# A state-space layer on one Trainium2 core: chunk kernels built inside the input-product loop, TensorE in a fixed order up to the gated unit, outputs by quarters, last blocks singly

## The chip, the cores and the metric

The kernel runs on one core of one Trainium2 chip, in one launch. The metric is the device time of one execution in microseconds. Five engines run their own instruction streams in order and wait for one another through semaphores: TensorE (PE: matrix products and transposes into PSUM), VectorE (DVE), ScalarE (ACT), GpSimd (POOL) and SyncE (SP, which here only issues DMAs). The DMAs of SP's queue bring the weights from HBM into SBUF.

## The reference

Two model blocks follow each other on 256 tokens of width 1024 in float32. The first has a state-space layer with its feed-forward part, then an attention layer with another. The second (a time-mixing layer, a differential attention, attention to a memory) is not touched. What the change touches is the first layer of the first block:

```python
shift1, scale1, gate1, shift2, scale2, gate2 = jnp.split(c_act @ ada_w[l] + ada_b[l], 6, axis=-1)
h = modulate(rms_norm(x, norm1_g[l]), shift1, scale1)
# s5_mixer, 64 groups of 16 channels, each with a 64-wide complex diagonal state
#   s_t = A s_(t-1) + B u_t ;  y_t = Re(C s_t) + d_skip * u_t
y = (y + d_skip.astype(f32) * h.astype(f32)).astype(h.dtype)
g = jax.nn.gelu(y)
mix = g * jax.nn.sigmoid(g @ w_glu + b_glu)
x = x + gate1[:, None, :] * mix
h = modulate(rms_norm(x, norm2_g[l]), shift2, scale2)
x = x + gate2[:, None, :] * swiglu(h, ffn_w_gate[l], ffn_w_up[l], ffn_w_down[l])
```

`c` is one vector, so `c_act @ ada_w` is a product of a vector with a 1024 x 6144 matrix (24 MB): it costs loading, hardly any arithmetic.

## The kernel before, in words

The state-space layer (`s5`) works on chunks of eight tokens. Its steps, in the order of the code:

1. *Input products.* For eight group sets `e`, DVE and POOL multiply the input matrix with powers of A (tile `P`, DVE's stream of 128x512 products), PE transposes the eight blocks of `P` (into `Bm`) and multiplies them with the output matrix `cbd`, which gives the response of a chunk to itself, `KTr`, a part of tile `x`.
2. *Inputs.* `xs` (tokens) are multiplied by a modulation that comes from the first 2048 columns of `ada_w` (tiles `in_adaH`), transposed into `U`, and turned into each chunk's contribution to the state: `into` (products `Bm`·`U`, copy `Gs`) and `turnG` (transposes, copies into `GT`).
3. *Scan.* DVE adds up the states over the 32 chunks: `St[:, 1::8] <- GT[:, 0::8]` first, then a recurrence of 45 instructions.
4. *Chunk kernels.* For four pairs `i`: two transposes of `KTr` by matrix product, to which a product with a 16x128 matrix adds `d_skip`; a copy; a split into two float32r parts `kparts` (ACT casts, POOL subtracts); 14 products with a shift matrix; ACT copies into `Kmat`.
5. *Outputs.* 64 products `Kmat`·`U` and 256 products `CE`·`St` add up in four PSUM banks `psY`; a copy to `ys`; transposes; gelu (`gT`) and its two parts `gh`, `gl`.
6. *Gated unit.* `proj` multiplies `w_glu` (four tiles of 1 MB, each cut into parts `whi`, `wlo`) with `gh`, `gl`: three products for each of 8 x 8 blocks, 192 in all. `evac` applies sigmoid, gate and residual, and the sums of squares for the next norm follow.

**The weight queue.** All big weights come as 128x2048 tiles `raw` (1 MB) through SP's queue, in program order, into a ring of three buffers. `deepen(3)` adds three more buffers, `rawq`, after the pool `old` has been closed; they lie in its memory, which holds `GT`, `xs`, `P`, `s5bc` and the scan's temporaries `w`. So the first DMA into `rawq` must wait for the scan's last instruction, and SP, which is in order, holds all later tiles behind it.

**The filler.** The vector-matrix products are cut into steps; `self.pump()` issues the next one: four products `ps_gv <- raw, crep` on one tile. The list is: `in_adaH` (8 tiles), two sets of `in_ada` (8 tiles each), `in_kvada` (on DVE and POOL: `acc <- raw, cs`, 8 tiles, under `issue_after(self.after)`), `in_ada1`.

**Order.** Tile's scheduler orders each engine's instructions by a cost model. Inside `tc.manual_schedule(engines={PE})` PE keeps the order of the code; before the change this reaches from the loop of step 1 to the last `turnG`. The scheduler chooses all the rest, among it where steps 4 to 6 stand.

The later parts that the change touches: `normed` and `ffn` (the feed-forward part, whose `self.after` holds back the DVE products of `in_kvada`), and `down`, its last projection (22 x 8 blocks, also by `proj`).

Of the kernel before, what the change touches and what calls it, by code (L numbers as in the profile page):

```python
# [9 lines left out]
F32 = mybir.dt.float32  # L10
# [125 lines left out]
def pack(inp):  # L136
# [40 lines left out]
    d = i["s5_d"][0].reshape(4, 2, 8, 16).transpose(2, 0, 1, 3).reshape(64, 16)  # L177
    dm = np.zeros((16, 64, 16), np.float32)
    dm[np.arange(16), :, np.arange(16)] = d.T
    a["s5d"] = dm.reshape(16, 1024)  # L180
# [108 lines left out]
class K:  # L289
# [135 lines left out]
    def proj(self, get, n0, kb, obs, xh, xl, evac, every=0):  # L425

        n = n0
        for o in range(0, len(obs), 2):
            ps = self.ps()
            pair = obs[o:o + 2]  # L430
            for e, ob in enumerate(pair):
# [202 lines left out]
    def s5(self):  # L634
# [3 lines left out]
        with ExitStack() as ctx:  # L638
# [17 lines left out]
            dd = x0[0:16, 4:8]  # L656
            G.dma_start(out=dd.rearrange("p a t -> p (a t)"), in_=a["s5d"])

            dm = dd.rearrange("p a (g e) -> p (a g) e", e=16)
# [152 lines left out]
            for h in range(2):  # L812
# [4 lines left out]
                for j4 in range(2):  # L817
# [5 lines left out]
                    (S_.copy if j4 else V.tensor_copy)(out=o, in_=pt)  # L823

# [24 lines left out]
            self.pipe(4, [into, turnG])  # L849
            order.close()  # L850
# [3 lines left out]
            scp = self.ps()  # L854
# [4 lines left out]
            V.tensor_copy(out=St[:, 1::8], in_=GT[:, 0::8])  # L859
# [26 lines left out]
            shift = sm.tile([128, 256], F32R, tag="junk", name="shift")  # L886
            S_.copy(out=shift[:, :240], in_=c["shift"])

            with ExitStack():
                for i in range(4):  # L890
                    pt = self.ps("aux")
                    for j in range(2):
                        self.mm(pt[:, 128 * j:128 * j + 128], KTr[:, 2 * i + j, :], self.ident, True, False)
                        self.mm(pt[:, 128 * j:128 * j + 128], self.ident[0:16, :],
                                dm[:, 16 * i + 8 * j:16 * i + 8 * j + 8].rearrange("p g e -> p (g e)"), False, True)
                    k7 = KM[i][:, 7].rearrange("p j n -> p (j n)")
                    S_.copy(out=k7, in_=pt[:, :256])
                    self.pump()
                    kp = sm.tile([128, 2, 256], F32R, tag="pm", name="kparts", bufs=2)
                    self.split(kp[:, 0], kp[:, 1], k7, G)  # L900
                    for t2 in (5, 3, 1, 0):
                        if t2 == 1 or t2 == 3 and i < 2:
                            self.pump()
                        pt = self.ps("aux")
                        ts_ = [0] if t2 == 0 else [t2, t2 + 1]
                        for e, tt_ in enumerate(ts_):
                            k = 7 - tt_
                            for p in range(2):
                                self.mm(pt[:, 256 * e:256 * e + 256], shift[:, 112 - 16 * k:240 - 16 * k], kp[:, p], p == 0, p == 1)
# [1312 lines left out]
```

## Time and profile before

| | |
|---|---|
| runs (us) | 1085.94, 1090.19, 1091.70; median 1090.19 |
| profiled execution (us) | 1090.09, its span 1088.3 |
| mean granted TensorE clock | 0.981 of full |
| busy share of the span | PE 91%, DVE 75%, ACT 54%, POOL 25% |
| the state-space stage, start to first product of the gated unit | 0 to 113.1 us |
| gated unit's products | 113.1 to 137.5 us |
| feed-forward part begins on PE | 144.8 us |

The page has the busy time of the engines, the span in forty slices, the DMA queues, the chain of work that ended last and the costliest groups of instructions. A timeline row has start, duration, engine and line, what is written from what, and the idle time in front with its releaser. PE's rows include idle gaps of its pipeline only where a bracket says so. The time of the execution outside the span is 1090.09 - 1088.3 = 1.8 us.

### The profile page before, as it was taken

Reading aid. Unit: us, or ns where it says so; the run is one execution under the profiler, and the core shown is the slowest. Engines: PE = TensorE matmul, PEld = TensorE weight load, DVE = VectorE, ACT = ScalarE, POOL = GpSimd, SP = SyncE. Lnnn points to the kernel's source line nnn. Section 1 sums busy time; section 2 is a strip of 40 time slices with the busy share of each in tenths; the row PEclk is TensorE's granted clock in tenths of the full one; section 3 lists DMA queues with packets and bytes.
Section 4 is the critical chain, followed back from the end, with each engine's and each line's share of the span. In section 5 each row is a group of like instructions: output and inputs, shape, how many; then the busy total and the mean of one; then the engine's idle time right before and its main releaser. Section 6 shows DMA issues by size and latency. Waiting matters only on the chain.

```text
span 1088.3 us, 21333 instructions
## 1 busy us (share of the span) xinstructions
PE 989.6 (91%) x8162; PEld 883.6 (81%) x8162; DVE 818.4 (75%) x1762; ACT 585.3 (54%) x1299; POOL 268.9 (25%) x302
## 2 busy tenths in 40 slices
PE   3889979989999888989999999988897989899996
PEld 1346869989999866878999999988787886699984
DVE  8856689889996887779665554689687835686995
ACT  6334655555544767656555544665444344474663
POOL 7960100020011550100000011453214232243331
PEclk9999989999999988999999999999999999899999
DMA  7985648887885251256655553332211233174421
GB/s 277 374 318 229 260 154 346 329 321 298 307 340 221 101 186 43 78 194 245 226 188 195 194 178 135 126 126 83 83 41 45 98 117 107 54 260 162 149 79 39
DMA packets 29414, 198.78 MB, mean 183 GB/s; under 512 B 3744, under 2 KB 3872, under 8 KB 6528
## 3 DMA queue, kind: packets, MB, share of 16 engines
q1 hardware_dynamic: 27936, 191.73, 47.6%
q10 hardware_dynamic: 720, 3.15, 0.8%
q0 software_dynamic: 656, 2.53, 0.7%
q8 instruction: 64, 1.05, 0.4%
q14 instruction: 38, 0.31, 0.1%
HBM read 195.31 MB, written 2.10 MB: 181 GB/s over the span
## 4 chain that ended last, share of the span: by engine, by line
PE 66%; DVE 16%; POOL 7%; issue 4%; ACT 3%; DMA 2%; SPq 0%; POOLq 0%; DVEq 0%; ACTq 0%
PE ps_mm L327 50%; PE ps_aux L327 6%; POOL CE L306 3%; DVE wlo L306 3%; PE ps_sv L327 3%; PE ps_st L327 2%; PE ps_aux L330 2%; PE ps_el L327 2%; POOL cem L306 2%; DMA raw<-in_ada 1%; DVE acc L323 1%; ACT whi L376 1%; DVE A L306 1%; DMA raw<-in_kvada 1%; POOL sq L306 1%
## 5 line engine op out<-in xcount | busy, mean ns | idle before, releaser
L376 ACT CAST whi<-raw 128x512 fp32r<-128x512 f32 (+2 forms) x488 | 296.4, 613 | 272.2 <-PE ps_mm L327 230.7
L306 DVE TENSOR_TENSOR wlo<-raw,whi 128x512 fp32r<-128x512 f32 (+2 forms) x412 | 289.8, 716 | 127.4 <-ACT whi L376 123.7
L327 PE MATMUL ps_mm<-hh,whi 128*128 128x256 f32 x1064 | 306.7, 289 | 3.4 <-ACT hh L298 2.3
L327 PE MATMUL ps_mm<-hh,wlo 128*128 128x256 f32 x1064 | 299.6, 284 | 3.5 <-DVE wlo L306 3.5
L327 PE MATMUL ps_mm<-hl,whi 128*128 128x256 f32 x1064 | 300.0, 283 | 0.7 <-DVE hl L323 0.3
L327 PEld LDWEIGHTS ps_mm<-hh,whi 128*128 128x128 f32 x1064 | 201.9, 190 | 7.8 <-ACT hh L298 2.9
L327 PEld LDWEIGHTS ps_mm<-hh,wlo 128*128 128x128 f32 x1064 | 200.4, 189 | 7.6 <-DVE wlo L306 5.8
L327 PEld LDWEIGHTS ps_mm<-hl,whi 128*128 128x128 f32 x1064 | 201.6, 190 | 2.2 <-DVE hl L323 1.4
L306 POOL TENSOR_TENSOR wlo<-raw,whi 128x512 fp32r<-128x512 f32 (+2 forms) x76 | 101.4, 1335 | 250.8 <-ACT whi L376 220.7
L306 POOL TENSOR_TENSOR sq<-sq 128x256 f32<-128x256 f32 x20 | 22.1, 1103 | 396.4 <-ACT sq L298 246.1
L327 PE MATMUL ps_mm<-ah,wlo 128*128 128x256 f32 x352 | 99.0, 282 | 0.0
L327 PE MATMUL ps_mm<-ah,whi 128*128 128x256 f32 x352 | 99.0, 281 | 0.0
L327 PE MATMUL ps_mm<-al,whi 128*128 128x256 f32 x352 | 98.8, 281 | 0.0
L323 DVE SCALAR_TENSOR_TENSOR acc<-raw,cs,acc 128x512 f32<-128x512 f32 x112 | 79.8, 756 | 2.1 <-DMA raw<-in_kvada 1.2
L327 PEld LDWEIGHTS ps_mm<-ah,wlo 128*128 128x128 f32 x352 | 66.3, 189 | 2.5 <-issue 1.7
L327 PEld LDWEIGHTS ps_mm<-ah,whi 128*128 128x128 f32 x352 | 67.3, 191 | 0.1
L327 PEld LDWEIGHTS ps_mm<-al,whi 128*128 128x128 f32 x352 | 66.4, 189 | 0.0
L327 PE MATMUL ps_gv<-raw,crep 128*32 128x512 f32 x192 | 28.8, 677 | 22.5 <-DVE ps_mm L306 14.4
L327 PEld LDWEIGHTS ps_gv<-raw,crep 128*32 128x32 f32 x192 | 4.8, 115 | 28.3 <-DVE ps_mm L306 14.4
L327 PE MATMUL ps_mm<-whi,ch 128*128 128x512 f32 x48 | 20.0, 448 | 1.2 <-ACT ch L422 1.2
L306 POOL TENSOR_TENSOR CE<-CE,cem 128x512 f32<-128x512 f32 x16 | 20.3, 1294 | 0.0
L327 PE MATMUL ps_mm<-oh,whi 128*128 128x256 f32 x64 | 20.1, 314 | 0.0
(554 smaller groups left out, 2063.4 us busy)
## 6 DMA issues: line engine op xcount, KB each, us to landing
raw<-in_gu SPq DMA_DIRECT2D x44, 1024.0 KB, 5.9
raw<-in_ada SPq DMA_DIRECT2D x32, 1024.0 KB, 7.1
raw<-in_dn SPq DMA_DIRECT2D x22, 1024.0 KB, 5.0
raw<-in_win SPq DMA_DIRECT2D x15, 1024.0 KB, 4.8
raw<-in_adaH SPq DMA_DIRECT2D x8, 1024.0 KB, 7.7
raw<-in_kvada SPq DMA_DIRECT2D x8, 1024.0 KB, 6.0
raw<-in_ada1h SPq DMA_DIRECT2D x8, 1024.0 KB, 6.4
raw<-in_wout SPq DMA_DIRECT2D x8, 1024.0 KB, 4.9
```

The costliest lines, as they stand in the source:

```text
L306: return (eng or self.nc.vector).tensor_tensor(out=out, in0=a, in1=b, op=op)
L323: return self.nc.vector.scalar_tensor_tensor(out=out, in0=a, scalar=s, in1=b, op0=op0, op1=op1, **kw)
L327: return self.nc.tensor.matmul(out, l, r, start=start, stop=stop, **kw)
L330: return self.nc.tensor.transpose(out, in_, self.ident)
L376: i = self.nc.scalar.copy(out=hi[:, :width], in_=raw[:, o:o + width])
```

## The change

- **Chunk kernels** (`kernels(i)`) are made inside the loop over `e` and, for the last pair, between the transposes of `xs`. The split is ACT's cast and a DVE subtraction straight from PSUM (POOL before). `d_skip` is added while `KTr` is made, by one more product per `e`, from a 128x128 matrix.
- **PE's fixed order** reaches up to the second half of gelu. Pumps: one per `e`, one between the halves of `xs`, one after each step of `into`/`turnG`, and **eight between the products `Kmat`·`U`**, which stand after `deepen(3)`.
- **Scan**: the copy into `St` goes to ACT, the gelu table is loaded ahead of it (`self.table`), the small PSUM tile has another tag.
- **Outputs by quarters**: `outputs(0..2)`, `gelu(0)`, `outputs(3)`, `gelu(1)`.
- **proj**: with `coming`, the first pair of blocks is done `k` by `k`, its 16 weight blocks taken first; with `single` the last block gets its own PSUM tile, and the block before it is evacuated alone. The gated unit has both, `down` has `single`.
- **`self.after`** is the last `lo` of the norm (`self.lowed`), not the last `nrm`.

```diff
-    def proj(self, get, n0, kb, obs, xh, xl, evac, every=0):
+    def proj(self, get, n0, kb, obs, xh, xl, evac, every=0, coming=False, single=False):
...
+            if coming and not o:
+                w = [get(n + i) for i in range(2 * kb)]
+                n += 2 * kb
+                for k in range(kb):
+                    for e in range(2):
+                        self.mm3(ps[:, e * T:(e + 1) * T], *w[kb * e + k], xh(k), xl(k), k + e == 0, k + e == kb)
+            for e, ob in enumerate(pair if o or not coming else ()):
+                if e and single and o + 2 >= len(obs):
+                    evac(pair[0], ps[:, 0:T])
+                    ps, pair = self.ps(), pair[1:]
+                    e = 0
...
+            def kernels(i):
+                pt = self.ps("aux")
+                for j in range(2):
+                    self.T(pt[:, 128 * j:128 * j + 128], KTr[:, 2 * i + j, :])
+                kp = sm.tile([128, 2, 256], F32R, tag="pm", name="kparts", bufs=2)
+                S_.copy(out=kp[:, 0], in_=pt[:, :256])
+                self.sub(kp[:, 1], pt[:, :256], kp[:, 0].bitcast(F32))
+                S_.copy(out=KM[i][:, 7].rearrange("p j n -> p (j n)"), in_=pt[:, :256])
+                yield
+                for t2 in (5, 3, 1, 0):
...
+                            self.mm(pt[:, 256 * e:256 * e + 256], shift[:, 112 - 16 * k:240 - 16 * k], kp[:, p], p == 0, p == 1)
...
+                yield
...
-                        self.mm(o, cbd[:, r, 4 * e + q].rearrange("p b e -> p (b e)"), pv(r, q), r == 0, r == 1, (0, 32 * q))
+                        self.mm(o, cbd[:, r, 4 * e + q].rearrange("p b e -> p (b e)"), pv(r, q), r == 0, False, (0, 32 * q))
+                self.mm(psK[:, 0:16], self.ident, dd[:, e], False, True)
                 S_.copy(out=KTr[:, e], in_=psK[:, :128])
-                self.pump(2 if e % 3 == 1 else 1)
+                if e % 2:
+                    kern = kernels(e // 2)
+                elif kern:
+                    next(kern)
+                self.pump()
+                if e % 2:
+                    next(kern)
...
+                if not h:
+                    next(kern)
+                    self.pump()
...
-            self.pipe(4, [into, turnG])
-            order.close()
+            for _ in self.steps(4, [into, turnG]):
+                self.pump()
+            self.table(AF.Gelu_apprx_tanh)
...
-            scp = self.ps()
+            scp = self.ps("aux")
...
-            V.tensor_copy(out=St[:, 1::8], in_=GT[:, 0::8])
+            S_.copy(out=St[:, 1::8], in_=GT[:, 0::8])
...
             first.close()
...
+                    if jp % 2:
+                        self.pump()
...
+            for i in range(3):
+                outputs(i)
+            gelu(0)
+            outputs(3)
+            gelu(1)
+            order.close()
...
-            self.proj(self.stream(a["wglu"]), 0, 8, list(range(8)), lambda k: gh[:, k], lambda k: gl[:, k], evac, 24)
+            self.proj(glu, 0, 8, list(range(8)), lambda k: gh[:, k], lambda k: gl[:, k], evac, 24, True, True)
...
-                self.stt(lo[:, k], t, s, hi[:, k].bitcast(F32), ALU.add, ALU.subtract)
+                self.lowed = self.stt(lo[:, k], t, s, hi[:, k].bitcast(F32), ALU.add, ALU.subtract)
...
-            self.after = self.scaled
+            self.after = self.lowed
```

The block of chunk kernels that stood behind the scan (step 4) is removed, with its pumps; `deepen(3)` stands between `first.close()` and the products `Kmat`·`U`, as before.

First, PE at the end of step 2 and in step 5. Before the change, behind the last `turnG` (`Gs` is its source):

```order
L330 MATMUL ps_aux<-c_cst_75,Gs 128x128 x4
L327 MATMUL ps_aux<-c_cst_75,x 128x128
L327 MATMUL ps_aux<-x,c_cst_75 128x128
L327 MATMUL ps_aux<-c_cst_75,x 128x128
L327 MATMUL ps_aux<-x,c_cst_75 128x128
L327 MATMUL ps_gv<-raw,crep 32x512 x4
L327 MATMUL ps_aux<-kparts,shift 128x256 x14
L327 MATMUL ps_gv<-raw,crep 32x512 x4
```

And now, from the last of the products `Kmat`·`U` (the first of eight such rows has `Kmat_242`) to the first `CE`·`St`:

```order
L327 MATMUL ps_mm<-Kmat_242,U 32x128 x8
L327 MATMUL ps_gv<-raw,crep 32x512 x4
L327 MATMUL ps_mm<-Kmat_243,U 32x128 x8
L327 MATMUL ps_gv<-raw,crep 32x512 x4
L327 MATMUL ps_mm<-Kmat_244,U 32x128 x8
L327 MATMUL ps_gv<-raw,crep 32x512 x4
L327 MATMUL ps_mm<-Kmat_245,U 32x128 x8
L327 MATMUL ps_gv<-raw,crep 32x512 x4
L327 MATMUL ps_mm<-CE_659,St 32x128 x2
```

These are the last four of eight pumps; all eight stand ahead of the first product `CE`·`St`. Before the change no pump stands between the last `Kmat`·`U` and the first `CE`·`St`.

Second, SP's queue around the transfer of the residual input `x` (brackets: semaphores waited for; `DVE_49` is the scan's last instruction in the row that also names `Pool_49`). Before:

```order
L925 DMA x<-in_xT 128x2048 [waits DMASW2_49,PE_49,Activation_49]
L357 DMA raw<-in_wglu 128x2048 [waits DVE_49,Activation_49,Pool_49]
L357 DMA raw<-in_wglu 128x2048
L357 DMA raw<-in_ada 128x2048 [waits DMAHW0_49]
L357 DMA raw<-in_wglu 128x2048 [waits DMAHW1_49]
L357 DMA raw<-in_ada 128x2048 [waits DMAHW2_49]
```

Now:

```order
L357 DMA raw<-in_ada 128x2048 [waits DVE_49,Activation_49,Pool_49]
L357 DMA raw<-in_ada 128x2048 x2
L357 DMA raw<-in_ada 128x2048 [waits DMAHW2_49,PE_49]
L357 DMA raw<-in_ada 128x2048 [waits DMAHW3_49,DMAHW1_49,PE_49]
L357 DMA raw<-in_ada 128x2048 [waits DMAHW4_49,PE_49]
L357 DMA raw<-in_ada 128x2048 [waits DMAHW5_49,PE_49]
L357 DMA raw<-in_ada 128x2048 [waits DMAHW6_49,PE_49]
L357 DMA raw<-in_wglu 128x2048 [waits DMAHW7_49,PE_49]
L357 DMA raw<-in_wglu 128x2048 [waits DMAHW0_49,PE_49]
L357 DMA raw<-in_ada 128x2048 [waits DMAHW1_49,PE_49]
L357 DMA raw<-in_wglu 128x2048 [waits DMAHW2_49,PE_49]
```

The row that follows is a tile of `in_kvada`. Before, 14 of the 16 tiles of `in_ada` were issued ahead of the wait for the scan; now 7 are, and 9 behind it.

Third, DVE in the loop of step 1, from the last products `P` of the seventh `e` to the modulation. Before:

```order
L306 TENSOR_TENSOR P<-P,ps_mm 128x512 x2
L306 TENSOR_TENSOR ps_mm<-ps_mm,s5bc 128x512
L306 TENSOR_TENSOR P<-ps_mm,s5bc 128x512
L306 TENSOR_TENSOR ps_mm<-ps_mm,s5bc 128x512
L306 TENSOR_TENSOR P<-P,ps_mm 128x512 x2
L323 SCALAR_TENSOR_TENSOR ps_mm<-ps_mm,modH 128x256
L306 TENSOR_TENSOR xs<-xs,ps_mm 128x1024 x4
```

Now:

```order
L306 TENSOR_TENSOR P<-P,ps_mm 128x512 x2
L306 TENSOR_TENSOR kparts<-ps_aux,kparts 128x256 x2
L306 TENSOR_TENSOR ps_mm<-ps_mm,s5bc 128x512
L306 TENSOR_TENSOR P<-ps_mm,s5bc 128x512
L306 TENSOR_TENSOR ps_mm<-ps_mm,s5bc 128x512
L306 TENSOR_TENSOR P<-P,ps_mm 128x512 x2
L323 SCALAR_TENSOR_TENSOR ps_mm<-ps_mm,modH 128x256
L306 TENSOR_TENSOR xs<-xs,ps_mm 128x1024 x3
L306 TENSOR_TENSOR kparts<-ps_aux,kparts 128x256
```

The subtractions of the second and third pair stand together, ahead of the last `e`'s products; the third pair's source on PE stands behind 14 shift products of the second pair and two pumps.

## Rows read from the trace of the kernel before

**Rows 1.** Windows: busy us of the engines (instructions), PE clock, DMA share, GB/s.
```profile
24.00:48.00 24.00, 21.61 (x242) 10.71 (x234) 23.93 (x38) 11.66 (x29) 23.53 (x34) 1.00 0.89 331
97.00:102.00 5.00, 5.00 (x192) 5.00 (x188) 0.69 (x1) 2.29 (x4) 0.00 (x0) 1.00 1.01 424
102.00:107.00 5.00, 3.67 (x80) 2.77 (x73) 2.78 (x5) 1.94 (x3) 0.00 (x0) 1.00 1.00 418
107.00:112.00 5.00, 2.58 (x20) 1.04 (x16) 2.39 (x7) 4.92 (x13) 0.00 (x0) 0.90 1.01 416
113.10:137.50 24.40, 24.40 (x203) 24.37 (x200) 15.04 (x26) 13.51 (x27) 4.42 (x5) 0.97 0.60 235
150.00:160.00 10.00, 8.22 (x65) 7.61 (x65) 10.00 (x19) 6.07 (x10) 0.00 (x0) 1.00 0.55 193
```

**Rows 2.** DVE's timeline, end of step 1 to the scan.
```profile
39.87 1.27 DVE L306 TENSOR_TENSOR P<-P,ps_mm 128x512 f32<-128x512 f32 x2
...
42.86 1.27 DVE L306 TENSOR_TENSOR P<-P,ps_mm 128x512 f32<-128x512 f32 x2
44.05 0.42 DVE L323 SCALAR_TENSOR_TENSOR ps_mm<-ps_mm,modH 128x256 f32<-128x256 f32 x1
44.51 4.86 DVE L306 TENSOR_TENSOR xs<-xs,ps_mm 128x1024 f32<-128x1024 f32 x4
...
68.19 4.39 DVE L859 COPY St<-GT 128x256 f32<-128x256 f32 x1 [1.93 <-ACT GT L846]
72.61 0.43 DVE L306 TENSOR_TENSOR ps_mm<-St,ps_mm 128x256 f32<-128x256 f32 x1
...
78.97 0.18 DVE L306 TENSOR_TENSOR mods<-ps_aux,c_cols 128x16 f32<-128x16 f32 x1 [0.87 <-PE ps_aux L628]
...
93.68 1.27 DVE L306 TENSOR_TENSOR St<-St,w 128x448 f32<-128x448 f32 x2
```

**Rows 3.** PE's timeline, steps 1, 2 and 4 (an x8 of `ps_gv` is one pump).
```profile
42.14 0.66 PE L327 MATMUL ps_aux<-P,cbd 128*32 128x128 f32 x16
42.67 1.07 PE L327 MATMUL ps_gv<-raw,crep 128*32 128x512 f32 x8
43.67 1.09 PE L330 MATMUL ps_aux<-c_cst,P 128*128 128x128 f32 x8
...
55.24 1.28 PE L327 MATMUL ps_aux<-Bm,U 128*32 128x128 f32 x32
...
62.84 1.06 PE L327 MATMUL ps_gv<-raw,crep 128*32 128x512 f32 x8 [1.05 <-DMA raw<-in_ada]
...
80.30 2.17 PE L327 MATMUL ps_aux<-kparts,shift 128*128 128x256 f32 x14
```

**Rows 4.** ACT's timeline: last GT copy, a small copy and cast, first weight part, table.
```profile
67.12 1.03 ACT L846 COPY GT<-ps_aux 128x256 f32<-128x256 f32 x2 [1.52 <-PE ps_aux L330]
68.59 0.37 ACT L897 COPY Kmat<-ps_aux 128x256 f32<-128x256 f32 x1 [0.43 <-PE ps_aux L327]
69.00 0.40 ACT L422 CAST kparts<-Kmat 128x256 fp32r<-128x256 f32 x1
...
99.89 1.69 ACT L376 CAST whi<-raw 128x512 fp32r<-128x512 f32 x3 [0.71 <-DMA raw<-in_wglu]
...
106.26 1.28 ACT L298 ACT_TABLE_LOAD   x1
107.56 1.09 ACT L298 ACTIVATE gT<-ps_aux 128x512 f32<-128x512 f32 x2
```

**Rows 5.** SP's timeline, the tiles behind the scan.
```profile
95.03 1.23 SPq L357 DMA_DIRECT2D raw<-in_wglu  x2
```

**Rows 6.** PE's timeline, steps 5 and 6.
```profile
96.48 6.66 PE L327 MATMUL ps_mm<-CE,St 64*32 64x128 f32 x229
...
107.54 1.33 PE L330 MATMUL ps_aux<-c_cst,ys 128*128 128x128 f32 x8
111.27 1.93 PE L327 MATMUL ps_gv<-raw,crep 128*32 128x512 f32 x8 [2.40 <-DMA raw<-in_ada]
113.13 0.58 PE L327 MATMUL ps_mm<-gh,whi 128*128 128x256 f32 x1
```

**Rows 7.** Chain that ended last, steps 3 to 6 and behind (start, us, what).
```profile
70.46 1.28 POOL CE L306
...
97.33 13.89 DMA raw<-in_ada
...
137.46 0.85 ACT sg L298 x2
138.31 0.02 issue
138.33 0.43 DVE sg L306
138.76 0.58 DVE x L323
...
150.07 1.35 DVE acc L319 x4
151.42 0.23 issue
151.65 0.69 DVE wlo L306
```

More of the change, by code (lines that the diff above doesn't have):

```diff
@@ L175, in pack @@
     a["s5bc"] = np.concatenate([lay3(i["s5_b_re"][0]), lay3(i["s5_b_im"][0]), lay3(cc[0]), lay3(cc[1])], 1)
[L177 to L180, printed above, removed]
+    d = i["s5_d"][0].reshape(4, 2, 8, 16).transpose(0, 1, 3, 2)
+    dm = np.zeros((4, 2, 16, 8, 16), np.float32)
+    dm[:, :, np.arange(16), :, np.arange(16)] = d.transpose(2, 0, 1, 3)
+    a["s5d"] = dm.reshape(128, 128)
     a["wglu"] = _blocks(i["s5_w_glu"][0])
@@ L655, in s5 @@
             x0 = self.xp.tile([128, 8, T], F32, name="x")
-            dd = x0[0:16, 4:8]
-            G.dma_start(out=dd.rearrange("p a t -> p (a t)"), in_=a["s5d"])
-            dm = dd.rearrange("p a (g e) -> p (a g) e", e=16)
+            G.dma_start(out=x0[:, 4, 0:128], in_=a["s5d"])
+            dd = x0[:, 4, 0:128].rearrange("p (g e) -> p g e", g=8)
             box = []
@@ L766, in s5 @@
             KTr = x0[:, 0:4].rearrange("p a (b n) -> p (a b) n", b=2)
+            shift = sm.tile([128, 256], F32R, tag="junk", name="shift")
+            S_.copy(out=shift[:, :240], in_=c["shift"])
+            def kernels(i):
[8 more added lines that the diff above has]
+                for t2 in (5, 3, 1, 0):
+                    pt = self.ps("aux")
+                    ts_ = [0] if t2 == 0 else [t2, t2 + 1]
+                    for e, tt_ in enumerate(ts_):
+                        k = 7 - tt_
+                        for p in range(2):
+                            self.mm(pt[:, 256 * e:256 * e + 256], shift[:, 112 - 16 * k:240 - 16 * k], kp[:, p], p == 0, p == 1)
+                    S_.copy(out=KM[i][:, t2:t2 + len(ts_)].rearrange("p t j n -> p (t j n)"), in_=pt[:, :256 * len(ts_)])
+                yield
             order = ctx.enter_context(ExitStack())
@@ L885, in s5 @@
                 self.add(o, o, w1[:, 1])
[L886 to L909, printed above, removed]
-                        S_.copy(out=KM[i][:, t2:t2 + len(ts_)].rearrange("p t j n -> p (t j n)"), in_=pt[:, :256 * len(ts_)])
             first.close()
@@ L924, in s5, with outputs @@
                                     KM[jp // 2][:, :, jp % 2, 32 * q + 16 * b:32 * q + 16 * b + 16], jp % 4 == 0, False, (0, r))
+                    if jp % 2:
+                        self.pump()
             nc.sync.dma_start(out=x0, in_=a["xT"].rearrange("p (k t) -> p k t", k=8))
-            for q2 in range(2):
-                for jp in range(8):
-                    y = psY[2 * q2 + jp // 4]
+            ys = B8("U", [128, 2, 8, 8, 16], "ys")
+            gT = B8("C", [128, 8, 8, 32], "gT", 4)
+            gh = B8("C", [128, 8, T], "gh", 4, F32R)
+            gl = B8("C", [128, 8, T], "gl", 4, F32R)
+            self.wparts, self.npart = [((_W(big, 4), "A"), (_W(big, 4), "CE"))], 0
+            glu = self.stream(a["wglu"])
+            def outputs(i):
+                y = psY[i]
+                for jp in range(4 * (i % 2), 4 * (i % 2) + 4):
                     for qo in range(2):
-                        g = 4 * jp + 2 * q2 + qo
+                        g = 4 * jp + 2 * (i // 2) + qo
                         for ri in range(2):
@@ L936, in s5, with gelu @@
                                         False, jp % 4 == 3 and ri == 1, (64 * b, r))
-            ys = B8("U", [128, 2, 8, 8, 16], "ys")
-            for i, y in enumerate(psY):
                 o = ys[:, i // 2, :, 4 * (i % 2):4 * (i % 2) + 4].rearrange("p t j e -> p j t e")
                 (V.tensor_copy if i % 2 else S_.copy)(out=o, in_=y.rearrange("p (j t e) -> p j t e", j=4, t=8))
-            gT = B8("C", [128, 8, 8, 32], "gT", 4)
-            gh = B8("C", [128, 8, T], "gh", 4, F32R)
-            gl = B8("C", [128, 8, T], "gl", 4, F32R)
-            self.wparts, self.npart = [((_W(big, 4), "A"), (_W(big, 4), "CE"))], 0
-            for q2 in range(2):
+            def gelu(q2):
                 for t4 in range(2):
@@ L1112, in down @@
             def down():
-                self.proj(self.stream(self.a[f"dn{l}"]), 0, 22, list(range(8)), lambda k: ah[:, k], lambda k: al[:, k], evac, 12)
+                self.proj(self.stream(self.a[f"dn{l}"]), 0, 22, list(range(8)), lambda k: ah[:, k], lambda k: al[:, k], evac, 12, single=True)
                 self.drain()
```

2 lines of the change are left out of this document (1 added, 1 removed).

## The prediction

> **What bounds the kernel now.** I read the windows first. In the input-product loop DVE is busy for 23.93 of 24 us and PE for 21.61 [rows 1]: the loop is a full DVE stream with a nearly full PE beside it. Then the timelines in the order of the stage. The loop's last products `P` end at 44.1, `xs` begins at 44.51, and after the copy into `St` (4.39 us) the scan runs from 72.61 to 94.95 [rows 2]. SP issues the first tile that must wait for the scan at 95.03 [rows 5]; its first weight part is cast at 99.89 [rows 4], 4.86 us after the issue. PE's products `CE`·`St` start at 96.48 and need no tile, but the last pump of `in_ada` waits until 111.27, and the gated unit starts behind it at 113.13 [rows 6]; the chain shows that tile as 13.89 us of DMA [rows 7]. From 113.1 to 137.5 PE has no gap (24.40 of 24.40) [rows 1]: 192 products, 24.4/192 = 0.127 us each. So three things set the end of the stage: DVE in the loop and the scan, six tiles behind the scan, and PE in the gated unit. All of it is on the path of the run, since the feed-forward part starts from its result.
>
> **The change part by part.** The sums stand against the profiled run (1090.09: span 1088.3 and 1.8 around it, which stays). It is 0.1 below the median, so I treat the two as one.
>
> *Loop.* DVE gets four subtractions of 128x256; none like them is in the loop's rows, the nearest of that size take 0.42 to 0.43 [rows 2], so 1.7 us in all, none of it hidden, as DVE is full. PE gets four times 14 shift products at 2.17 [rows 3] and two transposes (a quarter of the eight in 1.09, 0.3), 9.9 us, and loses three pumps of 1.07: +6.7 against 2.4 us of idle. Worse is the order. DVE takes the subtractions of the second and third pair together. The third one's source comes from PE behind the second pair's shift products, which need the second pair's subtraction. By the rows: the seventh `e` ends on DVE at 41.1 [rows 2], +0.4 for the first pair's subtraction, +0.4 for the second's, 42.0. Then PE: shift 2.17, pump 1.07, transposes 1.09, `cbd` 0.66, pump 1.07, two transposes 0.3 [rows 3], ACT's cast 0.40 [rows 4]: 48.8. DVE stands for 6.8 us. With the subtraction 49.2, and PE, which did the next `e` meanwhile, does 14 shift products and the pump that feeds the modulation (50.1 + 2.17 + 1.07 = 53.4); a copy on ACT, queued behind `Kmat` copies (about 1.1), and the modulation 0.42 [rows 2]: `xs` begins near 55 instead of 44.5, +10.5. `into` begins at 55.24 before [rows 3], 10.7 later; I take 65.0, +9.8, for some of the waits for tiles in between go.
>
> *To the scan.* From `into` to the last `GT` copy it is 55.24 to 68.15, 12.9 us [rows 3, 4], less the 1.05 of waiting for a tile [rows 3]: 76.9. Then ACT alone: table load 1.28, a tiny activation (0.2, an estimate), the copy into `St` (0.40, as its nearest neighbours of 128x256, 0.37 and 0.40) [rows 4]: the scan starts at 78.8 instead of 72.6. It loses the `mods` addition and its wait (0.87 + 0.18) [rows 2]: 22.3 - 1.05 = 21.3, end at 100.1, +5.1. The copy's 4.39 us goes, but it was long only beside POOL's stream, which ends at 71.74 [rows 7]. At 76.9 DVE would have been as quick, so I credit nothing beyond the sum. The Trainium skill (SBUF — State Buffer, "Who interferes with whom") says that a copy in DVE's two-port mode and GpSimd exclude each other for a whole instruction and that ACT waits for nobody; the 4.39 us agrees. By that rule the move to ACT has no worth once POOL is done, so the rule speaks against this part as the loop now stands.
>
> *Pumps ahead of the outputs.* This is the largest term. All eight pumps between `Kmat`·`U` stand ahead of the first `CE`·`St`, PE's order is fixed, and their first tile is the one whose DMA waits for the scan's last instruction. What queues behind them on PE is the whole rest of the stage. Tiles come at 2.50 us each by the windows' rate (1.049 MB at 416 to 424 GB/s) [rows 1], or at 2.83 by the pump that waited: fifth tile at 111.2, first at 99.9 [rows 4, 6], 11.3/4. I take 2.65. The eighth lands 4.86 + 7 x 2.65 = 23.4 after the scan, its pump takes 1.07: `CE`·`St` starts at 100.1 + 24.5 = 124.6 instead of 96.5. A page has a slower price: the Trainium skill (DMA: Bandwidth & Descriptors, "Specifications") gives a core about 358 GB/s of HBM, 2.93 us a tile. By it the thirteen tiles below would cost 3.4 us more; the 416 to 424 GB/s here contradict it.
>
> *Outputs, gelu, gated unit.* 192 of the products `CE`·`St` (6.66/229 each [rows 6]) 5.6, copy 0.6, four transposes 0.7 [rows 6], half of gelu 0.55 [rows 4], cast and subtraction 0.7: the first product of the unit at 132.8. The third needs a `wlo` that DVE makes behind four products `acc` of `in_kvada`, the thirteenth tile behind the scan: 100.1 + 4.86 + 12 x 2.65 = 136.8, then 1.35 [rows 7] and 0.69 [rows 7]: 138.8. Behind it on DVE stands the last quarter's copy (0.7), behind that the second half's transposes, gelu, cast and subtraction (1.1 + 1.1 + 0.7), near 143.5; 24 of the 192 products need only the first half, the other 168 take 21.3: end at 164.8 instead of 137.5, +27.3. Thus the quarters overlap hardly anything.
>
> *The rest.* `single` leaves one block of 256 where two were evacuated: 0.4 of ACT and 0.3 of DVE off the tail (0.85, 0.43, 0.58 [rows 7]), -0.7; in each of the two `down` 0 to -1, -0.5 each. One tile of `in_kvada` is already done: its 1.35 us, on the chain in the feed-forward part [rows 7], where DVE has no gap and PE 1.8 us of idle [rows 1], goes: -1.35. `self.lowed` only moves such work back by some tenths: 0, within 0.5 either way. Sum of the rest: -3.0.
>
> In all +27.3 - 3.0 = +24.3: **1114.4 us**. Bounds: the tile's price, 12 x (-0.15 to +0.18), -1.8 to +2.2; PE at the lower clock of 1.2 GHz after standing idle (a pump then took 1.93 instead of 1.07 [rows 3, 6]): 0 to +5.6 on the outputs; DVE's wait on `acc` not in the way: 143.5 becomes 138, -5.5. Own range 1107 to 1122.
>
> **Rivals.**
> *A. The loop hardly stalls*, because casts and transposes come earlier than my chain says. Then only the added work counts; `into` +1, `GT` at 68.1, scan 70.0 to 91.3, 8.8 earlier: 1106. For it: DVE alone has 1.7 us more. Against: the subtractions' place in DVE's order.
> *B. Faster: the outputs aren't held.* If the eight tiles were there when the scan ends, `CE`·`St` would start 1.5 us after it, as before (94.95, 96.48), at 101.6; first product of the unit 8.2 later, 109.8, end 134.2, -3.3, and -3.0 for the rest: 1084. It decides where the hold is under 6.3 us, hardly more than one landing (4.86). Against: the DMA's wait names the scan, and before, too, SP issued 0.1 us after it ended.
> *C. Slower still*: tiles at 2.83, the lower clock on outputs and transposes: +2.2 + 5.6 + 1.3: 1123.
> *D. No change*: hold and gains of the loop cancel; it needs a hold of 6 us: 1090.
>
> **How the numbers follow.** Forecast 0.58, A 0.20, B 0.06, C 0.13, D 0.03. About 0.5% (5.5 us) is what a measurement of this kernel can tell from no change. Slower 0.91, same 0.03, faster 0.06. The range 1100 to 1124 leaves out B, D and the tails of A and C.
>
> **What would show it.** Right: eight pumps in a row of waits for `in_ada`, ending some 24 us after the scan's end, `CE`·`St` only then; DVE idle for several us in the loop with ACT's cast as releaser; the copy into `St` on ACT near 0.4; a wait of PE for `wlo` early in the unit. Wrong: `CE`·`St` within 3 us of the scan's end, or pumps that find their tiles landed.

## The result and the profile after

The changed kernel takes 1117.68 us (median of 4 runs, 1117.00 to 1118.43); the kernel before, on the same chip, 1090.95 (4 runs). The ratio is 1.0244, 95% interval 1.0217 to 1.0270: slower by 26.7 us, where the prediction said 24.3; the time lies in the forecast's own range (1107 to 1122). The profiled execution is 1117.89 us, its span 1116.1, the mean granted clock 0.967.

| us from the start | before | predicted | after |
|---|---|---|---|
| `xs` begins on DVE | 44.51 | 55 | 57.68 |
| `into` begins on PE | 55.24 | 65.0 | 65.91 |
| last copy into `GT` ends | 68.15 | 76.9 | 77.15 |
| scan, first to last instruction | 72.61 to 94.95 | 78.8 to 100.1 | 78.99 to 99.40 |
| `CE`·`St` begins | 96.48 | 124.6 | 124.05 |
| first product of the unit | 113.13 | 132.8 | 134.07 |
| last product of the unit ends | 137.5 | 164.8 | 164.6 |
| feed-forward part begins | 144.8 | 171.4 (its delay of 26.6) | 172.53 |

The windows of after, to be laid beside [rows 1] (busy us of the engines in the same order, then the clock, DMA share and GB/s):

```profile
24.00:36.00 12.00, 9.69 (x82) 6.12 (x83) 12.00 (x21) 5.67 (x14) 11.53 (x22) 0.87 0.49 177
36.00:48.00 12.00, 11.76 (x99) 6.82 (x97) 5.98 (x11) 6.51 (x16) 12.00 (x13) 0.84 0.50 175
48.00:60.00 12.00, 11.61 (x124) 7.20 (x120) 6.13 (x9) 7.25 (x18) 12.00 (x11) 1.00 0.62 238
77.00:100.00 23.00, 1.35 (x24) 0.48 (x17) 19.34 (x48) 1.93 (x4) 0.00 (x0) 0.58 0.00 0
100.00:124.00 24.00, 14.52 (x180) 6.17 (x180) 0.17 (x1) 0.58 (x1) 0.00 (x0) 0.76 0.98 400
```

Two stretches stand out. From 36 to 60 us PE is full (23.37 of 24) and DVE, which bounded this stretch before, is busy for half of it. From 77 to 100 the DMA moves nothing: the seven tiles of `in_ada` that SP had issued are used by 77.9 us, the next tile's buffer lies in memory that the scan uses, and SP, which is in order, holds all later tiles behind it. From 100 to 124 it is the other way round: the DMA is full (0.98) and DVE and ACT have nothing to do.

PE's timeline of after, in the loop and from the scan to the unit (an x8 of `ps_gv` is one pump):

```profile
33.74 3.14 PE L327 MATMUL ps_aux<-kparts,shift 128*128 128x256 f32 x13 [2.07 <-DVE kparts L306]
36.81 1.94 PE L327 MATMUL ps_gv<-raw,crep 128*32 128x512 f32 x8
38.68 1.59 PE L330 MATMUL ps_aux<-c_cst,P 128*128 128x128 f32 x8
...
40.80 0.40 PE L327 MATMUL ps_aux<-x,c_cst 128*128 128x16 f32 x2
...
76.85 1.06 PE L327 MATMUL ps_gv<-raw,crep 128*32 128x512 f32 x8 [0.75 <-DMA raw<-in_ada]
...
104.54 1.93 PE L327 MATMUL ps_gv<-raw,crep 128*32 128x512 f32 x8 [26.19 <-DMA raw<-in_ada]
...
115.57 1.07 PE L327 MATMUL ps_gv<-raw,crep 128*32 128x512 f32 x8 [1.27 <-DMA raw<-in_ada]
...
123.05 1.07 PE L327 MATMUL ps_gv<-raw,crep 128*32 128x512 f32 x8 [0.99 <-DMA raw<-in_ada]
...
138.18 0.38 PE L327 MATMUL ps_mm<-gh,wlo 128*128 128x256 f32 x1 [2.25 <-DVE wlo L306]
```

SP issues the first of these tiles at 99.48, 0.08 us after the scan's last instruction; PE has by then stood for 21 us. The last four pumps come 2.49 us apart (115.57 to 123.05), and each waits 1.0 to 1.3 us for its tile; from the first to the fifth it is 11.03 us, 2.76 for each. `CE`·`St` needs none of them and stands behind the eighth.

DVE's timeline of after, in the loop, and where it holds up the sixth product of the unit (the third of its second block; the prediction calls it the third):

```profile
43.95 0.42 DVE L306 TENSOR_TENSOR kparts<-ps_aux,kparts 128x256 fp32r<-128x256 f32 x1 [1.11 <-ACT kparts L786]
...
52.14 0.43 DVE L306 TENSOR_TENSOR kparts<-ps_aux,kparts 128x256 fp32r<-128x256 f32 x1 [7.76 <-ACT kparts L786]
...
57.21 0.43 DVE L323 SCALAR_TENSOR_TENSOR ps_mm<-ps_mm,modH 128x256 f32<-128x256 f32 x1 [1.67 <-ACT ps_mm L674]
...
135.85 1.67 DVE L319 TENSOR_SCALAR acc<-raw,cs 128x512 f32<-128x512 f32 x4 [2.64 <-DMA raw<-in_kvada]
137.44 0.68 DVE L306 TENSOR_TENSOR wlo<-raw,whi 128x512 fp32r<-128x512 f32 x1
```

ACT's timeline of after, at the start of the scan:

```profile
76.14 1.01 ACT L890 COPY GT<-ps_aux 128x256 f32<-128x256 f32 x2 [0.90 <-PE ps_aux L330]
77.17 1.28 ACT L298 ACT_TABLE_LOAD   x1
78.46 0.20 ACT L298 ACTIVATE table<-eps 128x1 f32<-128x1 f32 x1
78.57 0.39 ACT L904 COPY St<-GT 128x256 f32<-128x256 f32 x1
```

### The profile page after: what moved, and what is told of

The parts are those of the page before. It is cut to its first block, busy times and chain, and to the rows that moved or that the text cites. A ratio compares the mean times of both kernels' runs of the same rounds, so it can differ in the third digit from the quotient of the medians.

```text
span 1116.1 us, 21301 instructions
## 1 busy us (share of the span) xinstructions
PE 990.8 (89%) x8154; PEld 886.5 (79%) x8154; DVE 815.6 (73%) x1765; ACT 584.3 (52%) x1301; POOL 264.0 (24%) x298
## 3 DMA queue, kind: packets, MB, share of 16 engines
q0 software_dynamic: 656, 2.53, 0.6%
## 4 chain that ended last, share of the span: by engine, by line
PE 69%; DVE 18%; issue 4%; ACT 4%; DMA 3%; POOL 1%; DVEq 0%; POOLq 0%; ACTq 0%; SPq 0%
PE ps_mm L327 50%; PE ps_aux L327 7%; PE ps_sv L327 3%; DVE wlo L306 3%; PE ps_aux L330 3%; PE ps_st L327 2%; PE ps_el L327 2%; DMA raw<-in_ada 2%; PE ps_gv L327 1%; DMA raw<-in_kvada 1%; DVE P L306 1%; ACT whi L376 1%; DVE A L306 1%; DVE ps_mm L306 1%; DVE Upr L306 1%
## 5 line engine op out<-in xcount | busy, mean ns | idle before, releaser
L327 PE MATMUL ps_mm<-gh,wlo 128*128 128x256 f32 x64 | 18.5, 293 | 2.5 <-DVE wlo L306 2.5
```

What stands on the lines that cost most here:

```text
L327: return self.nc.tensor.matmul(out, l, r, start=start, stop=stop, **kw)
```

## The experiments

All kernels ran beside runs of the kernel before, on the same chip (5 to 8 on another one than the rest). Milestones are those of the profiled executions, one for each kernel; times are medians.

### 1. The outputs ahead of the eight pumps

```diff
-                    if jp % 2:
-                        self.pump()
...
             gelu(1)
+            self.pump(8)
             order.close()
```

> The changed kernel with its eight pumps of in_ada moved from between the Kmat x U products to behind the second half of gelu, ahead of the gated unit; the tiles' order in SP's queue stays. Theory 1 (the tiles behind the scan are the price, 24.6 us for eight, then four more for in_kvada): CE x St starts 1.5 us after the scan's end, near 101, but the pumps then wait in front of the gated unit until about 124, and its third product still for the wlo behind in_kvada's tile (near 136): the unit ends 0 to 8 us earlier, 1110 to 1118. Theory 2 (the place of the pumps in PE's fixed order is the price, the tiles are there in time): the 23 us between scan and outputs go, 1095.

1108.17 us (1106.11 to 1109.67), ratio 1.0159 (1.0131 to 1.0188): 9.5 us of 26.7 come back, between the two theories. PE:

```profile
98.38 7.90 PE L327 MATMUL ps_mm<-CE,St 64*32 64x128 f32 x192 [18.08 <-DVE St L306]
...
123.67 1.89 PE L327 MATMUL ps_gv<-raw,crep 128*32 128x512 f32 x8 [2.73 <-DMA raw<-in_ada]
126.88 0.58 PE L327 MATMUL ps_mm<-gh,whi 128*128 128x256 f32 x1 [1.32 <-ACT whi L376]
```

`CE`·`St` now starts as the scan lets it, 26 us earlier, but the unit's first product only 7.2 us earlier: its tiles are queued behind the same eight. So moving the pumps out of the outputs' way gives back a third; the late start of the tiles stays, and experiment 2 takes that away.

### 2. The extra buffers later

The pumps stay where they were; `deepen(3)`, which sends the tiles into the scan's memory, moves behind them, and the ring starts anew there.

```diff
-            self.deepen(3)
...
 (behind the products Kmat.U and their eight pumps)
+            self.deepen(3)
+            self.nring = 0
```

> The changed kernel with deepen(3) moved behind the Kmat x U products and the ring started anew there, so that the eight pumped tiles go through the three old buffers and no tile of theirs waits for the scan; the order on PE, DVE and ACT is the same. Theory 1: the pumps end during the scan, CE x St starts 1.5 us after its end (101 instead of 124.05), in_kvada's tile lands near 107 and holds nothing, so that the unit's 168 late products follow at once: its end near 136.5 instead of 164.6, total 1088 to 1093. Theory 2 (the fixed order itself, whatever the tiles do): CE x St still starts over 15 us after the scan, total over 1108.

1092.35 us (10 runs), ratio 1.0010 (0.9989 to 1.0030): 25.3 of the 26.7 us are gone, with the same instructions in the same order on PE, DVE and ACT as far as the feed-forward part (behind it the scheduler moves some). PE:

```profile
78.21 1.06 PE L327 MATMUL ps_gv<-raw,crep 128*32 128x512 f32 x8 [0.98 <-DMA raw<-in_ada]
...
99.08 1.06 PE L327 MATMUL ps_gv<-raw,crep 128*32 128x512 f32 x8 [0.97 <-DMA raw<-in_ada]
100.07 3.28 PE L327 MATMUL ps_mm<-CE,St 64*32 64x128 f32 x104
```

The eight tiles run through the ring during the scan, and `CE`·`St` starts at 100.07, 1.8 us after the scan's end (98.24). (This execution, at 1095.36 us, is one of the slower of the ten, and one tile comes late in it: PE waits 3.18 us at 87.95. In experiments 7 and 8, with the same order up to there, `CE`·`St` starts at 98.31 and 98.29, 0.15 us behind the scan.) The loop still costs as much: in experiment 8 `into` begins 9.4 us later than before the change. But the scan ends only 3.2 later there, and the unit 0.8 earlier, so the rest of the change earns back what the loop costs. What hurts is neither the fixed order nor the pumps alone, but a fixed order that makes the outputs wait for tiles which themselves wait for the scan.

### 3. No tile of `in_kvada` in the unit

```diff
-            self.proj(glu, 0, 8, ..., evac, 24, True, True)
+            self.proj(glu, 0, 8, ..., evac, 48, True, True)
```

> The changed kernel with one pump instead of two in the gated unit (every 48 blocks, not 24): in_kvada's first tile goes to the feed-forward part. Theory 1: the third product no longer waits from 134.7 to 138.2, the last quarter's copy comes that much earlier, the unit ends 4 to 6 us earlier, and the tile's 1.4 us on DVE come back in the feed-forward part: 1112 to 1115. Rival (the second half of gelu is late because of the CE x St products and gelu themselves): no change, 1116 to 1119.

1112.50 us, ratio 1.0199 (1.0169 to 1.0229), 5.2 us less than the changed kernel; the unit ends at 158.0 instead of 164.6. Of these 6.6 us 2.3 lie ahead of the outputs (`CE`·`St` at 121.77 instead of 124.05), where the edit changes nothing: in this execution PE keeps its full clock in the loop (see the account of the loop below). From `CE`·`St` on 4.3 are left. So DVE's wait for this tile in front of the `wlo` of the sixth product costs 4 to 5 us.

### 4. The subtractions back on POOL

```diff
-                self.sub(kp[:, 1], pt[:, :256], kp[:, 0].bitcast(F32))
-                S_.copy(out=KM[i][:, 7]..., in_=pt[:, :256])
+                k7 = KM[i][:, 7].rearrange("p j n -> p (j n)")
+                S_.copy(out=k7, in_=pt[:, :256])
+                self.sub(kp[:, 1], k7, kp[:, 0].bitcast(F32), G)
```

> The changed kernel with the four subtractions of the chunk kernels on POOL, from ACT's copy in SBUF, instead of on DVE from PSUM. Theory 1 as the prediction had it (DVE's stand of 7 us in the loop delays xs): xs begins 6 to 9 us earlier, the total falls by as much, 1109 to 1112. Rival (PE is full in the loop since the change, and DVE's standing is only its shadow): the time follows what PE waits for POOL instead of DVE, between 3 us less and 5 us more, 1115 to 1123.

1124.59 us, ratio 1.0315 (1.0283 to 1.0346): 6.9 us slower than the changed kernel. DVE, then PE:

```profile
42.87 1.27 DVE L306 TENSOR_TENSOR P<-P,ps_mm 128x512 f32<-128x512 f32 x2
55.39 0.43 DVE L323 SCALAR_TENSOR_TENSOR ps_mm<-ps_mm,modH 128x256 f32<-128x256 f32 x1 [11.24 <-ACT ps_mm L674]
```

```profile
66.36 3.15 PE L327 MATMUL ps_aux<-kparts,shift 128*128 128x256 f32 x13 [6.71 <-POOL kparts L306]
```

DVE's stream `P` ends at 44.1 as before the change, and yet the modulation comes only at 55.39, 1.8 us earlier than after. The execution to compare with is that of experiment 3, where PE has the full clock in the loop as it has here, and DVE still subtracts:

```profile
54.32 0.43 DVE L323 SCALAR_TENSOR_TENSOR ps_mm<-ps_mm,modH 128x256 f32<-128x256 f32 x1 [1.67 <-ACT ps_mm L674]
```

There the modulation comes 1.1 us earlier than without DVE's subtractions. So DVE's standing wasn't the cause; it waited for PE, full with the added products. POOL's own stream then delays the last pair (6.71).

### 5. The chunk kernels during the scan

Experiment 2's kernel, with the kernels made behind the last `turnG` (subtractions on POOL, `k7` as above), four pumps between them, one pump per half of the outputs' products, and none in the unit.

```diff
-                if e % 2:
-                    kern = kernels(e // 2)
-                elif kern:
-                    next(kern)
-                self.pump()
-                if e % 2:
-                    next(kern)
+                self.pump(2 if e % 3 == 1 else 1)
...
+            ks = [kernels(i) for i in range(4)]
+            next(ks[0])
+            next(ks[1])
+            for i in range(4):
+                next(ks[i])
+                if i < 2:
+                    next(ks[i + 2])
+                self.pump()
```

> The kernel of e2 with the chunk kernels made behind the last turnG, while DVE scans (POOL subtracts, from ACT's copy), with the old two pumps for every third e, and without pumps in the gated unit; the rest of the change stays. Theory 1 (PE is full in the loop since the chunk kernels stand there, and each us of it delays xs, the scan and the outputs): xs begins at 45 to 48 instead of 57.7, the scan ends 6 to 9 us earlier than in e2, and with in_kvada out of the unit's way (4 us) the total is 10 to 13 less than e2's 1092.3: 1079 to 1083, faster than before. Rival (what leaves the loop comes back, since the chunk kernels with POOL's round trips are then done after the scan's end): CE x St starts over 4 us after the scan, 1086 to 1092.

1089.73 us (12 runs), ratio 0.9992 (0.9975 to 1.0009): a miss of 7 us. `xs` is back at 44.47 and the scan ends at 91.90, but the outputs are late:

```profile
83.59 1.65 PE L327 MATMUL ps_aux<-kparts,shift 128*128 128x256 f32 x6 [3.38 <-DVE St L306]
...
99.69 0.66 PE L639 MATMUL ps_aux<-c_cst,gemv 128*128 128x128 f32 x4 [0.71 <-ACT gemv L636]
100.28 3.94 PE L327 MATMUL ps_mm<-CE,St 64*32 64x128 f32 x134
```

The scan's small PSUM tile has the tag of the kernels' tiles, so a kernel waits there for `St` (3.38), and pumps stand among the last products before the outputs. The number is the rival's (`CE`·`St` 8.4 us after the scan); whether its cause is, POOL's round trips, experiment 9 asks, which takes away the wait and the pumps together.

### 6. The old pump pattern in the loop

Experiment 2's kernel with before's pumps in the loop.

```diff
-                self.pump()
+                self.pump(2 if e % 3 == 1 else 1)
```

> The kernel of e2 with the old two pumps for every third e, chunk kernels still in the loop. Theory 1 (PE's work in the loop is the price, not the order): xs may begin 2 us earlier, but into begins within 1 us of e2's, total within 2 us of e2's 1092.3. Rival (the modulation is late because its eighth pump stands two e later than before): xs and into come 4 us or more earlier, 1087 to 1088.

1102.02 us (4 runs, 1096.29 to 1105.46), ratio 1.0111 (1.0083 to 1.0140): 10 us slower than experiment 2, and than expected. `xs` begins at 54.01, 2.5 us earlier than there, `into` at 65.74, 1.0 later, as theory 1 says; the profiled execution, the fastest of the four, is 0.9 us longer than there. Why the others are longer still stays open.

### 7 and 8. Experiment 2's kernel without its `in_kvada` tile in the unit, and without `single`

```diff
-            self.proj(glu, ..., evac, 24, True, True)
+            self.proj(glu, ..., evac, 48, True, True)       (7)
+            self.proj(glu, ..., evac, 24, True)             (8; also in both down)
```

> The kernel of e2 with one pump instead of two in the gated unit, so that in_kvada's first tile goes to the feed-forward part. Theory 1: the product that waited for wlo behind in_kvada (113 to 116 in e2) goes on, the unit ends 3 to 5 us earlier, 1087 to 1090. Rival (with the tiles early the last quarter is late by itself): within 1 us of e2's 1092.3.

> The kernel of e2 without the single last block, in the gated unit and in both down projections. Theory 1 (the single block gains nothing in the gated unit, since ACT takes the block's sigmoid behind the squares of the block before it): from the unit's last product to the feed-forward part's first one it is 7.4 us, as before the change, against 7.9 in the changed kernel; total within 1.5 us of e2's 1092.3. The prediction's term: 0.7 more in the unit and 0.5 more in each down, 1.7 us slower in all.

7: 1092.13 us (ratio 1.0012); the unit ends 4.2 us earlier (138.15 against 142.31 at its last product's start), and nothing of that is left at the end: the rival's number, though not its reason. 8: 1092.41 (ratio 1.0031), against 1092.35 with `single`; from the start of the last product to the feed-forward part 8.20 against 8.17 us (from its end 7.9 in both, where 7.4 was expected without `single`). The times alone, 10 runs each on two chips, could not tell the 1.7 us of the prediction's term from nothing; the traces can. From the feed-forward part to the end, which holds both `down`, the two executions differ by 0.4 us. ACT in the changed kernel shows why `single` gives nothing:

```profile
165.70 0.42 ACT L298 ACTIVATE sq<-x 128x256 f32<-128x256 f32 x1 [1.57 <-DVE x L323]
166.02 0.46 ACT L298 ACTIVATE sg<-ps_mm,c_cols 128x256 f32<-128x256 f32 x1
```

The last block's product is done at 164.6, but its sigmoid `sg` stands on ACT behind the square of the block before, which waits for DVE.

### 9. Experiment 5 mended

```diff
-            scp = self.ps("aux")
+            scp = self.ps()
...
-                    if jp == 7:
-                        self.pump()
...
-            self.proj(glu, ..., evac, 0, True, True)
+            self.proj(glu, ..., evac, 24, True, True)
```

> The run with the chunk kernels made during the scan, mended at the two places that its trace named: the scan's small PSUM tile is taken from the other tag (a wait of 3.38 us for St stood there), no pump stands between the products CE.St, and two tiles of in_ada are pumped inside the gated unit again. Theory (those waits and the pumps alone kept the outputs back): scan end about 91.9 as there, CE.St at 93 to 95 instead of 100.28, last product of the unit at 128 to 130 instead of 133.89, total 1081 to 1086, faster than before. Rival (the kernels' casts, copies and subtractions themselves aren't done before 100): CE.St at 98 or later, 1086 to 1092, no difference from before.

1086.73 us (12 runs), ratio 0.9966 (0.9943 to 0.9989): 0.7 us above the expected range, where the rival's begins. In the stage the theory holds: the first `CE`·`St` starts at 91.91, 0.06 us behind the scan, and the unit ends near 130, 7.5 us earlier than before. But the lead shrinks to 0.9 us by 707 us, in the second block, which no edit touches. DVE, PE and POOL there:

```profile
686.62 6.02 DVE L1761 COPY Us<-c_cst 128x128 f32<-128x128 f32 x1
692.56 0.39 DVE L306 TENSOR_TENSOR hl<-nrm,hh 128x256 fp32r<-128x256 f32 x1
```

```profile
692.64 0.58 PE L327 MATMUL ps_mm<-hl,whi 128*128 128x256 f32 x1 [4.97 <-DVE Us L1761]
```

```profile
685.47 0.98 POOL L1649 MEMSET SAV<- 64x1024 f32 x1
...
691.54 0.98 POOL L1693 MEMSET BD<- 128x1024 f32 x1
```

The same copy is made three times; its group (ns, least, median and most):

```profile
L1761 DVE COPY Us<-c_cst x3: 215/217/6024, 686.6 to 812.9; 128x128 f32<-128x128 f32 x3
```

Twice it takes 0.22 us. Here, where the scheduler has put it ahead of other work, it stands beside a row of memsets on POOL and ends 0.1 us after the last; in the kernel before it stood later and took 1.18. Experiment 11's execution, with the same order there, shows it again: 6.03 us, ending 0.1 after POOL's row. (Five short instructions in front of it have the same end in the record, but each next one starts on time; only the one behind `Us` starts late, at 692.56.)

### 10 and 11. The copy into `St` on DVE again

In the changed kernel (10) and in experiment 9's (11):

```diff
-            S_.copy(out=St[:, 1::8], in_=GT[:, 0::8])
+            V.tensor_copy(out=St[:, 1::8], in_=GT[:, 0::8])
```

> The changed kernel with the copy GT -> St put back on DVE. Theory of the prediction (DVE's copy was long, 4.39 us, only beside POOL's stream, which is over by 72 us here): the copy takes 0.3 to 0.5 us at about 77, and the scan starts up to 1.5 us earlier than with ACT (table load and tiny activation no longer ahead of it); total within 2 us of 1117.7. Rival (the copy is slow on DVE by its strided operands, whatever POOL does): 4 us or more, scan 2 to 3 us later, total 1119 to 1121.

> The kernel with the chunk kernels made during the scan (mended), with the copy GT -> St on DVE instead of ACT. There the copy falls at about 69 to 70 us, beside POOL's stream for CE, if that still runs to about 71.7. Theory (DVE is long only beside POOL): 1.5 to 4.4 us, ending with POOL's stream. Rival (strided operands): 4 us or more even behind POOL's end; if it takes 0.5 us or less while POOL runs, both theories fall.

One run each: 1111.68 us and 1092.19. The copies on DVE, first of 10, then of 11, and POOL's last stream instruction in 11:

```profile
75.97 0.29 DVE L904 COPY St<-GT 128x256 f32<-128x256 f32 x1 [1.79 <-ACT GT L890]
```

```profile
69.69 2.12 DVE L898 COPY St<-GT 128x256 f32<-128x256 f32 x1 [1.86 <-ACT GT L884]
```

```profile
69.17 2.48 POOL L306 TENSOR_TENSOR CE<-CE,cem 128x512 f32<-128x512 f32 x2
```

0.29 us where POOL is done, 2.12 where it isn't, ending 0.16 after POOL's stream (71.65). In 10 the scan starts 2.7 us earlier than after, 1.2 of it from the loop (which the edit doesn't touch; PE's stretch at the lower clock is shorter in this execution) and 1.5 from the table load, which no longer stands ahead. Its total is 6.0 less than the changed kernel's, against 2 expected: a miss. 2.2 of the difference arise from the scan's start to the feed-forward part (a clock of 1.00 instead of 0.84 from 134 to 145 us); the rest stays open with one run.

### 12. The two copies mended

Experiment 9's kernel.

```diff
-                V.tensor_copy(out=U, in_=c["d16"]...)
+                S_.copy(out=U, in_=c["d16"]...)
...
-            self.table(AF.Gelu_apprx_tanh)
...
             S_.copy(out=St[:, 1::8], in_=GT[:, 0::8])
+            self.table(AF.Gelu_apprx_tanh)
```

> The mended kernel with the chunk kernels made during the scan, with two edits: the copy Us <- c_cst (in the second block) is on ACT instead of DVE, and the gelu table is loaded behind the copy into St instead of ahead of it. In that kernel's trace Us took 6.02 us on DVE (1.18 in the kernel before) beside a row of POOL's memsets, PE stood 4.97 us for it, and the lead over before shrank from 7.4 us at 488 us to 0.9 at 707. Theory (DVE's copy from SBUF to SBUF waits out POOL's stream, as the copy into St did): Us below 0.5 us on ACT, no wait of PE above 2 us there, 4.5 to 5.5 us back; the scan starts 1.3 us earlier, as the table load no longer stands before the copy; together 1079 to 1082 against 1086.7. Rival (DVE stands beside the memsets whatever it does there, so another of its instructions is slow in its place): only the 1.3 us of the table come, 1084.5 to 1086.5.

1084.50 us (9 runs, 1080.19 to 1089.56), ratio 0.9961 (0.9941 to 0.9982). ACT, and PE at the outputs:

```profile
681.64 0.30 ACT L1760 COPY Us<-c_cst 128x128 f32<-128x128 f32 x1
```

```profile
90.52 7.21 PE L327 MATMUL ps_mm<-CE,St 64*32 64x128 f32 x192 [1.94 <-DVE St L306]
```

Both mechanisms are as expected: `Us` takes 0.30, PE has no wait of even half a microsecond there, the stretch between the same two products of PE, from 485 to 698 us in this execution, is 5.8 us shorter than in experiment 9 (213.1 against 218.9; before 212.4), and the outputs start 1.4 earlier. The profiled run takes 1080.19, but the median of the timed ones misses the expected 1079 to 1082; the ratio is that of experiment 9 within the intervals. The two profiled executions differ by 9.1 us and the medians by 2.2: the one of experiment 9 is among its slower runs, this one is the fastest of its nine. What the other runs lose, the traces don't show. It has the lowest median of all, 0.4% under the kernel before and 33 us under the changed one, but is not clear of experiment 9.

## Why the prediction was right

**The hold of the outputs** (predicted 124.6, measured 124.05) is what experiments 1 and 2 show: 25.3 of 26.7 us go with the late tiles (in the profiled executions 22.1 of 27.7 at the start of the feed-forward part). Rival B, outputs not held, needed tiles that had landed; they are issued only when the scan ends. The price of a tile was 2.65 in the sum; from the first pump to the eighth it is 18.51 us, 2.64 for each of seven tiles. The first pump came 5.1 us after the scan where 4.86 were taken. So the hold, from the scan's end to `CE`·`St`, is 24.65 us for 24.5: mechanism and size were right. The lower clock, feared on the outputs with up to 5.6 us, cost nothing there: it rose during the pumps (granted 0.50 from 104 to 110 us, 1.00 from 112 on), and 192 products took 5.55 for the 5.6 of the sum.

**The loop** has the right size for a wrong reason, which is luck. The step "DVE stands for 6.8 us" because two subtractions stand together is seen (7.76), but experiment 4 takes it away and neither the modulation nor `into` comes earlier than in the like execution of experiment 3. PE is the bound there, and with the chunk kernels out of the loop (experiment 5) `xs` is back at 44.47. The sum gave PE +6.7 us and left out two things. The first is the eight pairs of products that add `d_skip`, in the diff as one line: their rows show 0.40, of which part overlaps with what follows; from start to start they take 0.24 to 0.33, 2.3 in all. 6.7 + 2.3 less the 2.4 of former idle is 6.6. The second is the clock behind PE's wait of 2.07 us (a pump 1.94, transposes 1.59 instead of 1.09). The same loop ran at full clock in experiment 3, behind a wait of 2.23. The window of after, then that of experiment 3 and its shift products:

```profile
34.00:38.00 4.00, 4.00 (x21) 2.79 (x21) 4.00 (x8) 2.13 (x5) 4.00 (x7) 0.50 0.01 4
```

```profile
34.00:38.00 4.00, 4.00 (x45) 2.66 (x43) 4.00 (x8) 2.84 (x6) 4.00 (x7) 1.00 0.09 16
```

```profile
33.56 1.81 PE L327 MATMUL ps_aux<-kparts,shift 128*128 128x256 f32 x13 [2.23 <-DVE kparts L306]
```

There `into` begins at 63.02, 7.8 us later than before the change (in experiments 1 and 2, with a shorter low stretch, at 64.7). So of the measured 10.7 us 2.9 are the lower clock of that one execution, and 7.8 the added work and its waits.

**The copy into `St`**: the prediction gave its move to ACT no credit for the 4.39 us [rows 2], since POOL is done by then, and experiment 10 confirms it: 0.29 on DVE. Behind the table load the move even costs 1.5 us. POOL's stream before the change ended one instruction later than the 71.74 that the prediction took, at 72.43, and the copy at 72.58:

```profile
71.68 0.75 POOL L306 TENSOR_TENSOR kparts<-Kmat,kparts 128x256 fp32r<-128x256 f32 x1
```

The Trainium skill (SBUF — State Buffer, "Who interferes with whom") lets one instruction of either engine block the other; the 2.12 us here and the 6.02 of `Us` agree on the lock, but DVE stood through several of POOL's instructions in a row, not one, as in the 4.39 us before.

**The unit** ended at 164.6 for 164.8, in part by luck: the terms behind 138.8 (0.7 + 1.1 + 1.1 + 0.7) add up to 142.4, not to 143.5, so that the sum as written ends at 163.7, and it had no lower clock there, while the granted clock was 0.50 from 140 to 142 us. The `acc` in front of `wlo` was put at 5.5 us as a bound and costs 4.3 to 5.2 (experiment 3).

**The failed term is "the rest, -3.0"**: the delay is 27.7 us at the start of the feed-forward part and 27.8 at the end. `single` was to give 0.7 and twice 0.5; experiment 8 gives it nothing in the unit and at most 0.4 in both `down` together, so far as two executions show; in the unit what ends last is ACT's order, not the size of the evacuated block. The 1.35 of an `in_kvada` tile done early was to come off the feed-forward part; no such gain is left at the end. (Experiment 3's gain in the unit stayed to the end, of experiment 7's 4.2 us nothing did; what decides that stays open.) Without this term the sum is 1117.4, and 1116.3 with its slip of 1.1 put right. `coming`, the quarters and `self.lowed` were not taken out one by one; what each of them is worth is not shown.

## What to carry to other kernels

When code is put into a fixed order on one engine, each filler in it becomes a wait: ask for every tile that it needs which buffer it goes to and what must end before that buffer is free. A filler that hangs on the work in front of it must not stand ahead of work that hangs on the same thing. And a gain in one stage has to be followed to the end: a scheduler's order far behind can move, and give it back, as `Us` did.

## What the runs showed of the hardware

- A DVE copy from SBUF to SBUF beside POOL's tensor products or memsets lasted until POOL's unbroken row of instructions ended: 4.39 us (to 0.15 us after it), 2.12 (to 0.16 after it), 6.02 and 6.03 (to 0.1 after it). With POOL idle it took 0.29 and 0.22, and 0.22 too beside a single POOL instruction of 128x4 elements, so not everything on POOL holds it. ACT's copy into `St` takes 0.39 with POOL idle (after) and 0.39 and 0.41 beside POOL's stream (experiments 9 and 12), its copy `Us` 0.30. DVE's copies out of PSUM in the same stretch (`Gs`, 0.69) show nothing of the kind.
- The weight queue, with one core of the chip at work, lands a tile of 1.049 MB every 2.49 us, 421 GB/s, at the last four of the eight pumps; from the first pump to the eighth it is 2.64 for each, since one step, from the fourth landing to the fifth, takes 3.7.
- The same 13 shift products at the same place of the loop took 3.14 us behind a wait of 2.07, 2.11, 2.53 and 2.40 behind 2.52 (experiments 1, 2 and 10), and 1.81 behind 2.23 and 2.26 (experiments 3 and 4). The granted clock fell to 0.50 in some of these executions and stayed at 1.00 in others, so the length of the wait alone doesn't decide it. A stall of 2 us in a full stream can cost up to 2.9 more, or nothing, and a comparison of two profiled executions has to look at that first.
